# Two fifths of the second group's modulation rows moved from VectorE to TensorE, state-space operands loaded earlier, and a new order at the second norm and at the end of a hybrid block

## The chip, the cores and the metric

The kernel runs on one core of a Trainium2 chip. The metric is the device time of one execution in microseconds. Three executions of the kernel before took 1408.05, 1410.48 and 1411.93 us, so its median is 1410.48 us.

## The reference

One block over 256 tokens of width 2048, all in float32:

```
mod = silu(c) @ w_ada + b_ada                      # 2048 x 12288; six vectors of 2048
sh1, sc1, g1, sh2, sc2, g2 = split(mod, 6)
h = rms_norm(x, norm_mix_g) * (1 + sc1) + sh1
u, q, k, v, ga, gb = split(h @ w_in)               # 2048 x 8192
y_ssm = s5_branch(u, ...)                          # state space: 64 groups of 16 channels, 64 states
y_att = moba_attention(q, k, v, rel_bias)          # 8 heads of 128, with a bias table
merged = sigmoid(ga) * (y_ssm @ w_proj_ssm) + sigmoid(gb) * (y_att @ w_proj_attn)
x = x + g1 * (merged @ w_out)
h2 = rms_norm(x, norm_mlp_g) * (1 + sc2) + sh2
x = x + g2 * (square(relu(h2 @ w_ff1)) @ w_ff2)    # 2048 x 8192 and back
return rms_norm(x, norm_final_g)
```

With 256 tokens each weight is used once per token, so the kernel is a stream of weights: every matrix is read once from memory.

## The kernel before, in words

**Weight tiles.** The weights come in tiles of 128 rows by 1024 columns of float32 (512 KB), issued on SyncE's queue into `wraw`, which has 7 buffers (L130 to 132). ScalarE rounds each tile to `whi` (L137) and VectorE forms the remainder `wlo` = tile − `whi` (L139). Each has 4 buffers. TensorE then makes three products of each tile: high activations by `whi`, low activations by `whi`, high activations by `wlo`. They are L174, L175, L176 where the result is transposed (`gemm_t`, 24 products of 256 columns for a tile), L271 to L273 (`gemm_n`, 512 columns), and L232 to L234 for the product before the second norm (`gemm_h`). I count weight tiles from 0 in the order in which they are used.

**Row tiles and groups.** The 2048 rows of the contraction are 16 row tiles. The normed activations `ah` and `al` of the row tiles are made in three groups of 4, 6 and 6 (`GR`, L52), since each row tile needs its scale and shift from `w_ada` first. A list in the body (L1050 to 1052) gives the order of the products over which group: first u, q, k, v over group 0 alone, that is weight tiles 0 to 15 with four row tiles each, then longer ones over groups 0 and 1, and so on. Weight tile 20 is the first that uses row tile 4, the first of group 1.

**The modulation.** There are two ways to multiply `w_ada` by `silu(c)`. `ada_first` (L279 to 309) reads loads of w_ada from `wan`, an arrangement with the contraction on the partitions. TensorE makes four products for each load (`adap`, L299), and after four loads ScalarE copies the sums and two small products (`adac`, L306) spread them. Row tiles 0 to 3 are done so, with 16 loads, ahead of or between the first weight tiles. `ada_job` (L311 to 333) reads rows from `wat`, and VectorE multiplies and sums each load in one instruction with an accumulator (L327). Group 1 takes 24 such loads and group 2 takes 24 more, and all the other vectors follow.

**Lanes.** Beside the stream run background jobs in lanes: "ada" (loads and products of w_ada, and the making of `ah`), "ssm" (the operands of the state-space branch, L567 to 660), and others. At each weight tile a lane earns a credit, its rate (`R1`, `R2`, `R3`, `SR1`, `SR2`), and spends it on its next jobs (L118). `need(g)` (L1034) makes sure that a group's activations are there and sets the next rates. `SL` empty jobs stand at the head of the ssm lane. From the order in which the code is written, and from priorities, a scheduler fixes the order of instructions on each engine, and at run time each engine keeps to it: an instruction that waits holds up all that stand behind it on its engine.

**State space.** The operands B and C come as `bt` and `ct`, one load each on SyncE's queue (L560, L562). VectorE makes complex products of them (L581 to 583, and `rt` in L635), TensorE transposes (`trv`, L618) and multiplies (`rk`, L651).

**Second norm and end.** `gemm_h` holds the products of the second 128 tokens (t = 1) of the last row tiles back, so that TensorE has work while the first 128 tokens' norm is made; the transposes `trh` (L1199) stand among them, after the scaling L1181. The last product is w_ff2, of which the last column half keeps three row tiles (`TF`) of each result bank for the very end. Behind it stand, for each result bank, L1300 (times g2), L1301 (plus x), L1302 (square and sum, ScalarE), then `final` (L1269 to 1281): sum of the squares, root, scaling of four pieces, two on VectorE (L1280) and two on ScalarE (L1278), and their stores, all on SyncE's queue.

Of the kernel before, what the change touches and what calls it, by code (L numbers as in the profile page):

```python
# [13 lines left out]
F32R = mybir.dt.float32r  # L14
# [10 lines left out]
H = 8  # L25
# [17 lines left out]
SR1 = .3  # L43
# [3 lines left out]
SL = 6  # L47
R1 = 1.65
R2 = .95
R3 = .5  # L50
# [3 lines left out]
GR = (4, 6, 6)  # L54
RAT = 1.5
RSS = .43
RPA = .65
RWO = .45
RM = .55
NP = 4  # L60
TW = 9
TF = 3
# [12 lines left out]
class Kern:  # L75
# [132 lines left out]
    def homes(self, at, tags):  # L208
# [7 lines left out]
        for tag in tags:  # L216
            n = 2 if tag in ("VT", "QT") else 1
            for j in range(n):
                out[at] = lambda tag=tag, j=j, n=n: pair(tag, j, n)
                at += 1  # L220
        return out

    def gemm_h(self, src, kts, c0, xh, xl, homes, tail, side=3, turns=((), ())):
# [12 lines left out]
        held = []  # L236
        for i, unit in enumerate(self.stream(src, kts, c0, homes)):
            for t in range(2):
# [3 lines left out]
                for s in range(2):  # L242
                    dot(t, s, i, *unit)
        yield banks
# [6 lines left out]
        yield banks  # L251

# [26 lines left out]
    def ada_first(self, j, half, done):  # L279
        nc = self.nc  # L280
        n = 2 * (1 - j) + half
        st = {}
# [8 lines left out]
        def total(i):  # L291
# [4 lines left out]
            with self.after(None if self.early else self.mm):  # L296
                for k in range(4):
                    q = 32 * k
                    self.adap = nc.tensor.matmul(p[q:q + 32, :], self.cz[:, 4 * i + k, :], w[:, k, :], start=i == 0,  # L299
                                                 stop=i == 3, tile_position=(0, q), skip_group_check=True)  # L300
            if i == 3:
                acc = self.s4[:, 512 + 256 * n:768 + 256 * n]
                nc.scalar.copy(acc, p)
                pc = self.tmp("adac")
                for k in range(2):
                    self.adac = nc.tensor.matmul(pc[:, k:k + 1], acc[:, k * P:(k + 1) * P], self.ones[:, 0:1],  # L306
                                                 start=True, stop=True)
                done(pc[:, 0:2])
        return [(lambda i=i: load(i), lambda i=i: total(i)) for i in range(4)]
# [142 lines left out]
    def bias_load(self):  # L452
        self.tz = self.slot("T", [P, H, S], name="tz")
# [102 lines left out]
    def ssm_load_bc(self):  # L556
        self.cmp = self.slot("S5", [P, 4, 32, 16], name="cmp")
        self.ct = self.slot("RT", [P, 2, 32, 16], name="ct")
# [208 lines left out]
    def ssm_start(self):  # L767
        self.rw = self.slot("SV", [P, 4, 512], name="rw")
        self.sri = self.slot("T", [P, 2, 2, 512], name="sri")
# [86 lines left out]
    def body(self):  # L856
        nc, a, v = self.nc, self.a, self.nc.vector
        with self.hot():
# [15 lines left out]
            v.tensor_copy(self.cz[:, :, 0], rc)  # L874
            self.ident = self.col("ident", P)
# [32 lines left out]
        def modn(half):  # L908
            return (self.ada_first(1, half, fin_scale(1, A1, lambda: self.gmix, 2 * half, 2))
                    + self.ada_first(0, half, fin_shift(0, B1, 2 * half, 2)))  # L910

# [138 lines left out]
        self.hop_in()  # L1050
        self.flush("ssm")
        self.bias_load()
# [345 lines left out]
```

## Time and profile before

| | |
|---|---|
| runs | 1408.05, 1410.48, 1411.93 us |
| the profiled execution | 1411.44 us, span 1409.3 us |
| TensorE busy | 1371.2 us, 97% |
| VectorE busy | 1056.0 us, 75% |
| ScalarE busy | 706.4 us, 50% |
| read from memory | 347.27 MB |

The span goes from the first instruction to the last, and the profiled execution took 2.1 us around it. PE is TensorE, DVE is VectorE, ACT is ScalarE, POOL is GpSimd and SP is SyncE. PEld is TensorE's weight load, and an engine's name with a q is its sequencer. "Busy" counts overlapping instructions once. In a row of a group, `x` gives the number of records, then come the busy time in us and the mean of one in ns. A transposed or small fp32 product leaves two records.

### The profile page before, as it was taken

To read this page: it belongs to the slowest core of one execution; us is meant where nothing else is said; L and a number is where in the kernel's file an instruction comes from. 1 tells how busy PE (TensorE), PEld (TensorE's weight loads), DVE (VectorE), ACT (ScalarE), POOL (GpSimd) and SP (SyncE) were. 2 spreads that over 40 slices of the span, in tenths; PEclk is the share of its full clock that TensorE was granted. 3 is DMA by queue.
4 is the path that set the end of the run, shared out by engine and by line. 5 is a ranking of instruction groups with operands and counts; after the bars stand their busy time and mean duration, and the time that the engine had idled before them with its cause. 6 is when DMAs were issued, how large, how long until landed. Compare 5 with 4: busy or idle time off the path is not lost.

```text
span 1409.3 us, 23394 instructions
## 1 busy us (share of the span) xinstructions
PE 1371.2 (97%) x9258; PEld 1221.7 (87%) x9258; DVE 1056.0 (75%) x1502; ACT 706.4 (50%) x937; POOL 40.9 (3%) x94
## 2 busy tenths in 40 slices
PE   7889999999999999999999999999999999999996
PEld 6789899899999999988788888888888888888885
DVE  5788989986799888978877776767676555655676
ACT  4454343366454853455655564545463544635444
POOL 1000000320000300000000000000000000000000
PEclk9999999999999999999999999999999999999998
DMA  9999987597457988887687677777767556565551
GB/s 349 373 382 363 318 293 233 159 299 241 149 186 257 316 294 297 296 335 276 229 298 269 209 262 239 254 247 268 264 220 263 186 188 195 176 203 191 183 203 60
DMA packets 113293, 353.19 MB, mean 251 GB/s; under 512 B 12080, under 2 KB 12096, under 8 KB 113056
## 3 DMA queue, kind: packets, MB, share of 16 engines
q1 hardware_dynamic: 110384, 347.13, 70.6%
q0 software_dynamic: 2800, 4.58, 1.1%
q8 instruction: 72, 1.18, 0.3%
q14 instruction: 37, 0.30, 0.1%
HBM read 347.27 MB, written 2.29 MB: 248 GB/s over the span
## 4 chain that ended last, share of the span: by engine, by line
PE 86%; DMA 6%; DVE 5%; ACT 1%; issue 1%; SPq 0%; DVEq 0%; ACTq 0%
PE pw L202 14%; PE pn L271 10%; PE pn L273 10%; PE pn L272 10%; PE pt L174 9%; PE pt L176 9%; PE pt L175 9%; PE pw L204 7%; DMA wraw<-in_w_in_dram 3%; DVE wlo L139 2%; DVE wraw L327 1%; PE pn L233 1%; PE pn L234 1%; PE pn L232 1%; DMA wraw<-in_wat_dram 1%
## 5 line engine op out<-in xcount | busy, mean ns | idle before, releaser
L137 ACT CAST whi<-wraw 128x1024 fp32r<-128x1024 f32 x443 | 461.9, 1052 | 553.5 <-PE pn L272 177.1
L139 DVE TENSOR_TENSOR wlo<-wraw,whi 128x1024 fp32r<-128x1024 f32 x443 | 538.3, 1223 | 255.8 <-ACT whi L137 252.9
L202 PE MATMUL pw<-mh,whi 128*128 128x512 f32 x896 | 311.5, 396 | 0.2 <-DVE part L1260 0.2
L174 PE MATMUL pt<-ah,whi 128*128 128x256 f32 x896 | 251.4, 288 | 7.2 <-ACT whi L137 5.1
L175 PE MATMUL pt<-ah,whi 128*128 128x256 f32 x896 | 250.3, 285 | 0.0
L204 PE MATMUL pw<-mh,wlo 128*128 128x256 f32 x896 | 243.0, 280 | 1.0 <-DVE wlo L139 1.0
L176 PE MATMUL pt<-ah,wlo 128*128 128x256 f32 x896 | 237.7, 286 | 2.8 <-DVE wlo L139 2.5
L327 DVE SCALAR_TENSOR_TENSOR wraw<-wraw,cb 128x1024 f32<-128x1024 f32 x176 | 213.6, 1220 | 0.0
L272 PE MATMUL pn<-whi,ff 128*128 128x512 f32 x512 | 199.3, 389 | 0.0
L271 PE MATMUL pn<-whi,ff 128*128 128x512 f32 x512 | 198.6, 390 | 0.0
L202 PEld LDWEIGHTS pw<-mh,whi 128*128 128x128 f32 x896 | 165.4, 188 | 36.3 <-issue 0.5
L273 PE MATMUL pn<-wlo,ff 128*128 128x512 f32 x512 | 185.4, 389 | 0.0
L174 PEld LDWEIGHTS pt<-ah,whi 128*128 128x128 f32 x896 | 172.1, 193 | 10.8 <-ACT whi L137 6.8
L204 PEld LDWEIGHTS pw<-mh,wlo 128*128 128x128 f32 x896 | 168.8, 188 | 5.5 <-DVE wlo L139 1.4
L175 PEld LDWEIGHTS pt<-ah,whi 128*128 128x128 f32 x896 | 172.6, 193 | 0.7 <-DVE ah L139 0.2
L176 PEld LDWEIGHTS pt<-ah,wlo 128*128 128x128 f32 x896 | 164.7, 193 | 4.8 <-DVE wlo L139 4.4
L271 PEld LDWEIGHTS pn<-whi,ff 128*128 128x128 f32 x512 | 96.1, 188 | 20.0 <-issue 0.2
L273 PEld LDWEIGHTS pn<-wlo,ff 128*128 128x128 f32 x512 | 96.1, 188 | 20.1
L272 PEld LDWEIGHTS pn<-whi,ff 128*128 128x128 f32 x512 | 96.1, 188 | 19.6
L1294 DVE TENSOR_TENSOR y<-y,pn 128x512 f32<-128x512 f32 x48 | 30.9, 683 | 14.8 <-PE pn L273 14.8
L271 PE MATMUL pn<-whi,mh 128*128 128x512 f32 x96 | 37.7, 392 | 0.0
L272 PE MATMUL pn<-whi,mh 128*128 128x512 f32 x96 | 37.4, 390 | 0.0
(400 smaller groups left out, 1658.1 us busy)
## 6 DMA issues: line engine op xcount, KB each, us to landing
wraw<-in_w_ff_dram SPq DMA_DIRECT2D x256, 512.0 KB, 4.7
wraw<-in_wat_dram SPq DMA_DIRECT2D x176, 512.0 KB, 5.5
wraw<-in_w_in_dram SPq DMA_DIRECT2D x128, 512.0 KB, 5.3
wraw<-in_w_out_dram SPq DMA_DIRECT2D x32, 512.0 KB, 6.3
wraw<-in_wan_dram SPq DMA_DIRECT2D x16, 512.0 KB, 8.7
wraw<-in_w_proj_attn_dram SPq DMA_DIRECT2D x16, 512.0 KB, 6.2
wraw<-in_w_proj_ssm_dram SPq DMA_DIRECT2D x16, 512.0 KB, 5.8
wraw<-in_w_glu_dram SPq DMA_DIRECT2D x8, 512.0 KB, 5.0
```

What stands on the lines that cost most here:

```text
L137: h = self.nc.scalar.copy(hi, src)
L139: s = self.nc.vector.tensor_sub(lo, src, hi.bitcast(F32))
L174: nc.tensor.matmul(o, hi[:, c], xh[:, kx, :], start=st, stop=False, skip_group_check=True)
L175: nc.tensor.matmul(o, hi[:, c], xl[:, kx, :], start=False, stop=False, skip_group_check=True)
L176: self.mm = nc.tensor.matmul(o, lo[:, c], xh[:, kx, :], start=False, stop=sp, skip_group_check=True)
L202: nc.tensor.matmul(banks[b], hi[:, c], x2[:, k0 + k].rearrange("p h s -> p (h s)"), start=i + k == 0, stop=False, skip_group_check=True)
L204: self.mm = nc.tensor.matmul(banks[b][:, 0:S], lo[:, c], x2[:, k0 + k, 0, :], start=False, stop=i == n - 1 and k == 1, skip_group_check=True)
L271: nc.tensor.matmul(o, xh[:, kx, tk], hi[:, c], start=q == 0, stop=False)
L272: nc.tensor.matmul(o, xl[:, kx, tk], hi[:, c], start=False, stop=False)
L273: self.mm = last = nc.tensor.matmul(o, xh[:, kx, tk], lo[:, c], start=False, stop=q == n - 1)
L327: v.scalar_tensor_tensor(w, w, 1.0, self.cb[:, (i % 2) * 1024:(i % 2 + 1) * 1024], op0=OP.mult, op1=OP.mult, accum_out=pc[:, i:i + 1])
L1294: v.tensor_add(d, d, banks[b])
```

## The change

**The start.** `PP` gives the second group's row tiles 6 to 9 (as quarters 3 and 4 of the columns) to `ada_first`. 16 of the 24 loads of group 1 then go to TensorE. For these the small products are units of their own (`spread`), and the operand `cz2` and the sums lie in a new tile, `rt0`, of which `ct` takes the other part. `mod1` keeps row tiles 4 and 5. The two kinds of unit are merged evenly.

```diff
-SR1 = .3
+SR1 = .7
-SL = 6
-R1 = 1.65
+SL = 3
+R1 = 1.8
-R3 = .5
+R3 = .25
+PP = ((), (3, 4), ())
-RPA = .65
-RWO = .45
-RM = .55
+RPA = .75
+RWO = .65
+RM = .75
...
         for g in range(1, len(GR)):
             k0, n = groups[g]
-            chain += self.ahead(mod1(k0, n)) + [hjob(k0 + i) for i in range(0, n, 2)]
+            rows = mod1(k0, n - 2 * len(PP[g]))
+            cols = sum([modp(2 + sum(PP, ()).index(q), 2 * q) for q in PP[g]], [])
+            units = [u for _, _, u in sorted([((i + .5) / len(z), m, u) for m, z in enumerate((rows, cols))
+                                              for i, u in enumerate(z)], key=lambda e: e[:2])]
+            chain += self.ahead(units) + [hjob(k0 + i) for i in range(0, n, 2)]
...
-            mid = {1: lambda: second(0), 2: lambda: second(1)} if (which, g0) == (0, 0) else (lambda: need(g1)) if g1 > g0 else None
+            mid = {1: lambda: second(0), 2: lambda: second(1)} if (which, g0) == (0, 0) else {groups[g1][0] - kts[0]: lambda: need(g1)} if g1 > g0 else None
...
-        self.hop_in()
         self.flush("ssm")
         self.bias_load()
+        self.hop_in()
```

With the larger `SR1` and the smaller `SL`, the loads of `bt` and `ct` stand after weight tile 4 instead of weight tile 19. On SyncE's queue, with `in_w_in` for weight tiles and `in_wat` and `in_wan` for w_ada, this is where the two loads stood before (weight tiles 17 to 19 are the three in one row):

```order
L320 DMA wraw<-in_wat_dram 128x1024
L132 DMA wraw<-in_w_in_dram 128x1024 x3
L560 DMA cmp<-in_bt_dram 128x1024
L562 DMA ct<-in_ct_dram 128x1024
L320 DMA wraw<-in_wat_dram 128x1024
```

And this is where they stand now; the `in_w_in` row ahead of `bt` is weight tile 4:

```order
L358 DMA wraw<-in_wat_dram 128x1024
L132 DMA wraw<-in_w_in_dram 128x1024
L318 DMA wraw<-in_wan_dram 128x1024 x2
L132 DMA wraw<-in_w_in_dram 128x1024
L598 DMA cmp<-in_bt_dram 128x1024
L318 DMA wraw<-in_wan_dram 128x1024
L600 DMA rt_85<-in_ct_dram 128x1024
L358 DMA wraw<-in_wat_dram 128x1024
```

Before weight tile 20 stand 68 loads of this size in both kernels. The state-space work on VectorE moves with its operands. On VectorE, the stretch from the last product of group 1's modulation (the rows with `cb`) to the first activations of row tile 4 (`ah`) read so before:

```order
L327 SCALAR_TENSOR_TENSOR wraw,pc<-wraw,cb 128x1024 x2
L139 TENSOR_TENSOR wlo<-wraw,whi 128x1024
L429 TENSOR_TENSOR xt<-xt,R 128x512
L331 TENSOR_TENSOR pcs<-pc 128x6
L139 TENSOR_TENSOR wlo<-wraw,whi 128x1024
L429 TENSOR_TENSOR xt<-xt,R 128x512
L894 TENSOR_TENSOR B_113<-pcs,cols 128x6
L139 TENSOR_TENSOR wlo<-wraw,whi 128x1024
L635 TENSOR_TENSOR rt<-id_105,d_93 128x2048
L139 TENSOR_TENSOR ah<-htmp,ah 128x2x256
```

Now it reads as follows; L619 to L621 and L673 are state-space work:

```order
L621 TENSOR_TENSOR tt<-cmp,AB 128x512
L139 TENSOR_TENSOR wlo<-wraw,whi 128x1024
L467 TENSOR_TENSOR xt<-xt,R 128x512
L369 TENSOR_TENSOR pcs<-pc 128x2
L139 TENSOR_TENSOR wlo<-wraw,whi 128x1024
L467 TENSOR_TENSOR xt<-xt,R 128x512
L621 TENSOR_TENSOR bp<-tt 128x32x16
L937 TENSOR_TENSOR B_117<-adac,cols 128x2
L673 TENSOR_TENSOR rt<-id_109,d_97 128x2048
L937 TENSOR_TENSOR B_117<-pcs,cols 128x2
L139 TENSOR_TENSOR wlo<-wraw,whi 128x1024 x2
L365 SCALAR_TENSOR_TENSOR wraw,pc<-wraw,cb 128x1024
```

After these twelve rows come one more `wlo`, one more L365 and then `ah`. The last product of group 1's own modulation stands directly ahead of them; the two L365 belong to group 2. On TensorE, the 64 added `adap` products stand in fours and eights between weight tiles 2 and 18. The 128 `trv` transposes move from weight tiles 64 and 65 to weight tiles 29 to 44, the 128 `rk` products from weight tiles 67 and 68 to weight tiles 49 to 52.

**Slots.** `tz` (the bias table's rows), `sri` and `yl` change from the buffer "T" to "S5", `yatt` and `sg` the other way.

**Second norm.** In `gemm_h` the products held back for t = 1 are issued after the last product of the stream, and the ada lane stops for the last eleven tiles of w_out's second column half:

```diff
-            with self.after(self.turned[at[0]] if at else None):
+            with self.after(self.turned[at[0]] if at else last):
...
         for i, unit in enumerate(self.stream(src, kts, c0, homes)):
+            if i == n - tail - 2:
+                self.lanes["ada"][1] = 0.0
```

**The end.** The last column half of w_ff2's last eight row tiles goes through a new function, `gemm_e`: t = 0 is computed whole first, then t = 1 in pieces of 512, 256 and 256 columns, with the last four weight tiles kept in a larger "AHL" buffer. The steps behind the product keep their form (`last2`), so t = 0's final scaling stands ahead of t = 1's results, and two of t = 1's four stores go to ScalarE's queue.

```diff
+        first = [(self.bank("pe0"), slice(0, 512)), (self.aux("pe1"), slice(512, 1024))]
+        held = []
+        for i, unit in enumerate(self.stream(src, kts, c0, homes)):
+            held.append((i,) + unit)
+            for o, c in first:
+                dot(o, 0, c, *held[-1])
+        last = self.mm
+        yield first
+        then = []
+        for name, c in (("pe2", slice(0, 512)), ("pe3", slice(512, 768)), ("pe4", slice(768, 1024))):
+            o = (self.aux(name) if name == "pe3" else self.bank(name))[:, 0:c.stop - c.start]
+            for u in held:
+                dot(o, 1, c, *u, last=last)
+            then.append((o, c))
+        yield then
...
-                nc.sync.dma_start(self.out[0, t * P:(t + 1) * P, cc], o)
+                    q = nc.sync if t == 0 or c in (0, 2) else nc.scalar
+                    q.dma_start(self.out[0, t * P:(t + 1) * P, cc], o)
```

VectorE's rows before, from the last result bank (`pn_13461`) to the sum of t = 1's squares; L399 to L402 are the small steps of t = 0's root:

```order
L1300 TENSOR_TENSOR y_9010<-pn_13461,g2b 128x512
L399 RECIPROCAL r30s<-r30s 128x1
L1301 TENSOR_TENSOR x<-x,y_9010 128x512
L400 SCALAR_TENSOR_TENSOR r30t<-r30s 128x1
L401 TENSOR_TENSOR r30t<-r30t,r30v 128x1
L402 SCALAR_TENSOR_TENSOR r30s<-r30t,r30s 128x1
L1280 SCALAR_TENSOR_TENSOR x<-x,r30s,gfb 128x512 x2
L1272 TENSOR_REDUCE fs_13637<-fq 128x1
```

And now, where `r30s` is the root of t = 0, `r31s` that of t = 1, and `pe_13701` the last piece of 256 columns:

```order
L1331 SCALAR_TENSOR_TENSOR x<-x,r30s,gfb 128x512 x2
L1339 TENSOR_TENSOR y_9087<-pe_13651,g2b 128x512
L1340 TENSOR_TENSOR x<-x,y_9087 128x512
L1339 TENSOR_TENSOR y_9087<-pe_13676,g2b 128x256
L1340 TENSOR_TENSOR x<-x,y_9087 128x256
L1339 TENSOR_TENSOR y_9087<-pe_13701,g2b 128x256
L1340 TENSOR_TENSOR x<-x,y_9087 128x256
L1323 TENSOR_REDUCE fs_13735<-fq 128x1
```

The two scalings of t = 0 stood between the last result and the sum of its squares, and now stand ahead of all of t = 1's results.

More of the change, by code (lines that the diff above doesn't have):

```diff
@@ L251, in gemm_h, with gemm_e, dot @@
         yield banks
+    def gemm_e(self, src, kts, c0, xh, xl, homes, koff):
+        nc = self.nc
+        n = len(kts)
+        def dot(o, t, c, i, kt, hi, lo, last=None):
+            tk, kx = slice(t * P, (t + 1) * P), kt - koff
+            with self.after(last):
+                nc.tensor.matmul(o, xh[:, kx, tk], hi[:, c], start=i == 0, stop=False)
+            nc.tensor.matmul(o, xl[:, kx, tk], hi[:, c], start=False, stop=False)
+            self.mm = nc.tensor.matmul(o, xh[:, kx, tk], lo[:, c], start=False, stop=i == n - 1)
+        first = [(self.bank("pe0"), slice(0, 512)), (self.aux("pe1"), slice(512, 1024))]
[4 more added lines that the diff above has]
+                dot(o, 0, c, *held[-1])
+        last = self.mm
+        yield first
[6 more added lines that the diff above has]
+        yield then
     def gemm_n(self, src, kts, c0, xh, xl, koff=0, tail=1):
@@ L281, in ada_first @@
         n = 2 * (1 - j) + half
+        cz = self.cz if half < 2 else self.cz2
         st = {}
@@ L298, in total, with spread @@
                     q = 32 * k
-                    self.adap = nc.tensor.matmul(p[q:q + 32, :], self.cz[:, 4 * i + k, :], w[:, k, :], start=i == 0,
+                    self.adap = nc.tensor.matmul(p[q:q + 32, :], cz[:, 4 * i + k, :], w[:, k, :], start=i == 0,
                                                  stop=i == 3, tile_position=(0, q), skip_group_check=True)
             if i == 3:
-                acc = self.s4[:, 512 + 256 * n:768 + 256 * n]
-                nc.scalar.copy(acc, p)
-                pc = self.tmp("adac")
-                for k in range(2):
[L306 to L309, printed above, removed]
+                st["acc"] = (self.s4[:, 512 + 256 * n:768 + 256 * n] if half < 2 else
+                             self.rt0[:, 1536 + 256 * j:1792 + 256 * j])
+                nc.scalar.copy(st["acc"], p)
+                if half < 2:
+                    spread()
+        def spread():
+            pc = self.tmp("adac")
+            with self.after(None if half < 2 else self.mm):
+                for k in range(2):
+                    self.adac = nc.tensor.matmul(pc[:, k:k + 1], st["acc"][:, k * P:(k + 1) * P],
+                                                 (self.ones if half < 2 else self.one)[:, 0:1], start=True, stop=True)
+            done(pc[:, 0:2])
+        units = [(lambda i=i: load(i), lambda i=i: total(i)) for i in range(4)]
+        return units if half < 2 else units + [(lambda: None, spread)]
     def ada_job(self, vec, k0, n, done):
@@ L1265, in ff1 @@
                     self.split(f[:, 0, s], f[:, 1, s], fr[:, s])
-        fq = self.col("fq", 8)
+        fq = self.col("fq", 9)
         def final(t):
@@ L1280, in final, with last2 @@
                         v.scalar_tensor_tensor(o, o, rf, gfb[:, cc], op0=OP.mult, op1=OP.mult)
[L1281 removed]
+                    q = nc.sync if t == 0 or c in (0, 2) else nc.scalar
+                    q.dma_start(self.out[0, t * P:(t + 1) * P, cc], o)
+        def last2(t, o, c, q, keep=None):
+            keep = keep or (lambda ins: ins)
+            d = acc[:, t, c]
+            with self.hot():
+                keep(v.tensor_mul(d, o, g2b[:, c]))
+                keep(v.tensor_add(x1[:, t, c], x1[:, t, c], d))
+                nc.scalar.activation(d, x1[:, t, c], AF.Square, accum_out=fq[:, q:q + 1])
         def ff2(g):
             f = ffs.pop(g)
[L1285 to L1287 removed]
+            for cg in range(1 if g == 7 else 2):
+                banks = self.gemm_n(w2, range(8 * g, 8 * g + 8), cg * 1024, f[:, 0], f[:, 1], koff=8 * g)
                 for b in range(4):
```

51 lines of the change are left out of this document (27 added, 24 removed).

## The prediction

> **What bounds the kernel now.** I read the page first, then the windows of the first 380 us, then the chain and TensorE's timeline where a window shows loss. The page says that TensorE sets the time almost everywhere:
>
> ```profile
> PE 1371.2 (97%) x9258; PEld 1221.7 (87%) x9258; DVE 1056.0 (75%) x1502; ACT 706.4 (50%) x937; POOL 40.9 (3%) x94
> ```
>
> So the change can save only what TensorE idles, what it does at a lower clock, and the tail behind it. The windows of the start show where that is (columns: window, its length, busy time of PE, PEld, DVE, ACT, POOL, granted clock, DMA share, GB/s):
>
> ```profile
> 42.00:104.00 62.00, 55.48 (x387) 50.12 (x388) 53.67 (x75) 29.23 (x41) 0.00 (x0) 1.00 1.01 387
> 104.00:192.00 88.00, 83.51 (x603) 79.29 (x603) 78.75 (x112) 37.76 (x43) 0.00 (x0) 0.96 0.87 317
> 192.00:380.00 188.00, 184.73 (x1900) 179.26 (x1899) 155.36 (x232) 95.17 (x154) 19.65 (x40) 0.98 0.71 232
> ```
>
> Up to 104 us the DMA is full (1.01) and TensorE idles 6.5 of 62 us. From 104 to 192 us VectorE is nearly full, 78.75 of 88, and TensorE idles 4.5. From 192 to 380 us VectorE has 32.6 us to spare, TensorE idles 3.3 us and runs at a clock of 0.98. The borders are weight tiles, by the timeline of TensorE (start, duration): weight tiles 20, 48 and 100 are first used with their `wlo` at
>
> ```profile
> 104.17 0.39 PE L176 MATMUL pt<-ah,wlo 128*128 128x256 f32 x1
> 192.09 0.28 PE L176 MATMUL pt<-ah,wlo 128*128 128x256 f32 x1
> 380.16 0.28 PE L176 MATMUL pt<-ah,wlo 128*128 128x256 f32 x1
> ```
>
> I count the sum in these three times, which I call T20, T48 and T100. After T100 the streams are alike until the second norm.
>
> **The start, up to weight tile 20.** The prices of an instruction among its like are in the chain (start, duration) and the groups:
>
> ```profile
> L299 PE MATMUL adap<-wraw,tz 128*32 128x256 f32 x128 | 8.2, 384 | 0.9 <-DMA wraw<-in_wan_dram 0.8
> 38.42 0.62 PE adac L306 x4
> 742.58 1.23 DVE wraw L327 x2
> 743.81 1.15 DVE wlo L139
> 240.20 1.13 DVE tt L583
> 249.75 0.61 DVE tt L583
> ```
>
> VectorE loses 16 L327 at 1.23 us, 19.7 us. TensorE gains as many `adap` as it has now, 8.2 us, and four groups of `adac` at 0.62: 10.7 us. That is 4.2 more than the 6.5 it idles there, so by TensorE alone T20 would be at most 104.2 + 4.2 = 108.4. The number of loads before weight tile 20 stays 68, so the full DMA lands that tile at the same time. What decides is VectorE's order. Now, by its timeline, the activations of row tile 4 follow 9.3 us behind the start of group 1's last L327, and `rt` in between waits 1.07 us for ScalarE's copy of `ct`:
>
> ```profile
> 93.02 1.22 DVE L327 SCALAR_TENSOR_TENSOR wraw<-wraw,cb 128x1024 f32<-128x1024 f32 x1
> 100.09 2.29 DVE L635 TENSOR_TENSOR rt<-id,d 128x2048 f32<-128x2048 f32 x1 [1.07 <-ACT cc L567]
> 102.30 0.68 DVE L139 TENSOR_TENSOR ah<-htmp,ah 128x512 fp32r<-128x512 f32 x1
> ```
>
> The early operands take that wait away. But in the new order there stand between the same two places five wlo, two L327 of group 2, two state-space steps, `rt` and two `xt`: 5 x 1.15 + 2 x 1.23 + 0.61 + 0.61 + 2.29 + 2 x 0.61 = 12.9 us, 13.5 with the smallest. The last load of group 1 is number 63 in the order of loads, 61 before; a load of 524 KB at 387 GB/s takes 1.35 us, so its L327 starts at about 95.7 and ends at 96.9. `ah` then starts at 110.4. The other bound is the load of weight tile 22, number 71, whose wlo stands ahead of `ah`: three loads (4.1 us) behind weight tile 20, whose wlo starts at
>
> ```profile
> 102.98 1.14 DVE wlo L139
> ```
>
> which is 101.9 without the wait of 1.07 before `rt`. Then 101.9 + 4.1 + 1.15 + 1.23 = 108.4 is the least for `ah`. If that wait stays, 110.4 becomes 111.5, about 112. I take 110 for `ah` and so for T20, 6 us later than now. TensorE then waits some 2 to 6 us at weight tile 20, which it does not do now. Now it waits one tile later:
>
> ```profile
> 108.81 0.39 PE L176 MATMUL pt<-ah,wlo 128*128 128x256 f32 x1 [1.49 <-DVE wlo L139]
> ```
>
> **From weight tile 20 to 48.** VectorE's new order holds, from `ah` to weight tile 48's wlo, 26 wlo (29.9 us), 22 L327 (27.1), 12 state-space steps of 1.13 (13.6), and 29 short ones at 0.61 (12 more state-space steps, 12 evacuations, 5 on `xt` and `ah`: 17.7), together 88.3, with the smallest some 88.5. The old order filled 78.75. TensorE needs 83.51 at a clock of 0.96, 80.2 at full clock, and the transposes moved here:
>
> ```profile
> L618 PE MATMUL trv<-ident,bp 64*64 64x64 f32 x256 | 7.9, 219 | 0.0
> ```
>
> That is 88.1, so TensorE and VectorE are level here, and any idle of VectorE counts. It idles 9.25 of 88 us now, for loads among other things:
>
> ```profile
> 151.20 8.25 DMA wraw<-in_w_in_dram
> 159.56 1.06 ACT whi L137
> 160.66 0.58 PE pt L174
> ```
>
> I take 2 us of idle, because a fuller VectorE leaves loads more time (ends: 0 and all 9.25), and 1.5 for TensorE's half tile behind it. T48 = 110 + 88.5 + 2 + 1.5 = 202.0, against 192.1: 9.9 us later.
>
> **From 48 to 100: paid back.** The transposes are gone from here, 7.9 us. VectorE's work falls from 155.4 to about 120 us by the same count, while TensorE's is 184.73 x 0.98 − 7.9 = 173, so VectorE is not late for the `rk` products as it is now:
>
> ```profile
> 255.00:260.00 5.00, 1.73 (x13) 1.41 (x12) 4.97 (x5) 1.58 (x4) 0.00 (x0) 0.81 0.00 0
> 260.00:266.00 6.00, 6.00 (x126) 5.78 (x124) 5.15 (x9) 2.69 (x5) 0.00 (x0) 0.59 0.78 244
> ```
>
> The chain leads through L581 to L583 into ScalarE's L641 and then to `rk`. TensorE idles 3.3 us of the first window, then runs 6 us at 0.59, which loses 2.5: 5.8 in all. The loads start earlier, so VectorE's results lie ready and I count the whole 5.8 as gone. Sum: 7.9 + 5.8 = 13.7. T100 is 9.9 − 13.7 = **3.8 us earlier**. With other ends: `ah` at 108.5 and no idle give −7.3; `ah` at 112 and 5 us of idle give +1.2. The two removed waits, on `ct` and at `rk`, are thus mostly bought with a new one at weight tile 20.
>
> [...] First the rows: after waits of 0.26, 0.76 and 1.98 us TensorE ran at 0.51 for 6 us,
>
> ```profile
> 155.00:160.00 5.00, 2.66 (x13) 1.66 (x11) 4.16 (x8) 1.49 (x2) 0.00 (x0) 0.91 1.03 415
> 160.00:166.00 6.00, 5.34 (x25) 5.35 (x26) 6.00 (x9) 2.70 (x3) 0.00 (x0) 0.51 0.89 309
> 160.66 0.58 PE L174 MATMUL pt<-ah,whi 128*128 128x256 f32 x1 [1.98 <-ACT whi L137]
> ```
>
> so a spell costs 6 x 0.49 = 2.9 us, and the new wait at weight tile 20 should bring one. TensorE's 88.1 and these 2.9 are 91.0, within the 92.0 us from 110 to 202, so it adds nothing to the sum; in A it adds 2.9 at most. [...]
>
> **Slots, bias table, other rates.** Moving `tz`, `sri`, `yl`, `yatt` and `sg` between two buffers, and the bias table ahead of `hop_in` on GpSimd's queue, I cost at nothing: GpSimd is 3% busy. If a buffer came free late, TensorE would wait a few us before 400 us; this lies in the range.
>
> **Second norm.** TensorE waits 1.17 us at the first transposes:
>
> ```profile
> 678.55 0.50 DVE xs L1181
> 679.18 1.06 PE L1199 MATMUL trh<-ident,xs 128*128 128x128 f32 x8 [1.17 <-DVE xs L1181]
> ```
>
> VectorE is late there by its L327. In the new order no L327 stands among the last eleven splits of w_out, where six stood: 7.4 us less on VectorE, more than the 1.17. The transposes should not wait, with what the pipeline refills −1.3. The L327 left out come later, where this chain shows VectorE as the last to end (two of its rows, 742.58 and 743.81, stand above); if they press there, 1 us comes back.
>
> **The end.** After TensorE's last product the chain now reads
>
> ```profile
> 1398.37 0.69 DVE y L1300
> 1399.13 0.66 DVE x L1301
> 1400.28 1.42 DVE x L1280 x2
> 1401.69 0.08 DVE fs L1272
> ```
>
> and in the timeline ScalarE's square and the eight stores are
>
> ```profile
> 1399.82 0.63 ACT L1302 ACTIVATE y<-x 128x512 f32<-128x512 f32 x1 [1.22 <-DVE x L1301]
> 1401.06 4.50 SPq L1281 DMA_DIRECT2D out_dram<-x  x8
> ```
>
> The sum of squares of t = 1 waits for t = 0's scaling, 1.42 us, and comes 1401.69 − 1398.37 = 3.3 us behind the product. In the new order that scaling is done earlier, and the last piece has 256 columns, so the three steps 0.69, 0.66 and 0.63 take somewhat over half, and with the accumulator's read some 1.7: −1.6. TensorE pays: 24 products of 512 columns become 48 of 256. Their steps are
>
> ```profile
> 1397.20 0.23 PE pn L272
> 1397.42 0.23 PE pn L273
> 380.04 0.28 PE L175 MATMUL pt<-ah,whi 128*128 128x256 f32 x1
> ```
>
> 0.227 us over many such rows, and 0.12 (to 380.16): 48 x 0.12 − 24 x 0.227 = +0.3. Eight stores take 4.50 us to issue, 0.56 each with its wait; two of the last four on another queue save about half of one, −0.3. Sum −1.6. `gemm_e` needs t = 0's last weights no later than now, and keeps four tiles, so I see no new wait; if there is one, TensorE waits 1 to 2 us.
>
> **The sum.** −3.8 − 1.3 − 1.6 = −6.7. The profiled execution took 1411.4 us and would take 1404.7; it lies 0.96 above the median of 1410.48, and against that I predict **1403.8 us**. A measurement of this kernel can tell about 0.3% from no change, 4.2 us: below 1406.3 is faster, above 1414.7 slower.
>
> **The rivals.**
> - Forecast, 0.48: VectorE sets T48, rests after it, and the sum is 1400 to 1407.
> - A, larger gain, 0.17: `ah` comes near 105, because VectorE, relieved of 19.7 us, runs through its rows as loads land. Then TensorE is the bound: T48 = 105 + 88.1 = 193, one us later than now, and less 13.7 the start gives −12.7; in all −15.6, 1394.9, with 1392 to 1398. For it: VectorE's 53.67 of 62 us loses more than a third. Against it: the new order puts weight tile 22's wlo ahead of `ah`.
> - B, moved only, 0.22: the change doesn't do what it says, since VectorE's state-space work lands in the stretch where it was nearly full. `ah` at 112 and 5 to 6 us of idle make T48 207.5 to 208.5, and the start +2: 1409.6, with 1406 to 1413. For it: the 78.75 of 88.
> - C, slower, 0.13: VectorE's idle does not shrink, because the loads arrive as late as now and every split waits behind an L327 that waits for its load. With `ah` at 114 and all 9.25 us of idle, T48 is 213.3, 21 later; less 13.7 the start is +7.5 and the total +4.6: 1415. It decides from about 9 us of idle on. For it: a DMA share of 0.87 there. Against it: the total of loads is unchanged, and 22 L327 take the place of 24.
>
> Faster is A and most of the forecast, 0.60; same the rest of it and B, 0.27; slower C, 0.13. The range leaves out C and the far part of A: 1394 to 1413.
>
> **What would show it.** In the profile after: a first use of weight tile 20 near 110 us with a wait on `ah` or its wlo; VectorE over 85 of 88 us busy from there to weight tile 48; no wait at `rk`, and a clock near 1.00 from T48 to T100; weight tile 100 at 376; the wait at `trh` gone; some 1.7 us from the last product to the last sum of squares. I am wrong if T20 stays near 104 (A), or if VectorE idles over 5 us between weight tiles 20 and 48 (B, C).

## The result, and the profile after

The changed kernel takes 1422.91 us (median of 4), against 1409.57 for the kernel before on the same chip: a ratio of 1.0093, interval 1.008 to 1.0106. It is slower by some 13 us, 0.9%, and 1 lies outside the interval; 1403.8 was forecast and 1413 was the upper end. (16 of group 1's 24 loads moved, which is two thirds of the second group's rows and not the two fifths of the title.) The profiled execution took 1422.08 us (span 1420.2), 10.6 us more than that of before; the page of the kernel after begins its busy times with

```profile
PE 1385.2 (98%) x9426; PEld 1227.4 (86%) x9426; DVE 1038.8 (73%) x1479; ACT 706.4 (50%) x944; POOL 41.3 (3%) x95
```

VectorE is relieved, by 17 us, as the change says, and TensorE is busy 14 us more. To see where the time went I mark the moments by which TensorE has done 20, 53, 69, 101, 200 and 250 weight tiles' worth of products. Lateness of the kernel after at these marks: 7.4, 28.9, 6.4, 6.4, 8.0 and 10.6 us; at TensorE's last product 12.2, and at the end of the span 10.9. The 28.9 is mostly the state-space products, which now lie ahead of mark 53 and not behind it. Windows between the first marks, of the kernel before (window, length, busy PE, PEld, DVE, ACT, POOL, clock, DMA share, GB/s):

```profile
0.00:103.10 103.10, 86.14 (x626) 72.88 (x627) 73.76 (x180) 47.02 (x68) 5.29 (x21) 0.98 0.98 371
103.10:205.40 102.30, 97.81 (x722) 93.59 (x721) 92.49 (x128) 46.26 (x54) 0.00 (x0) 0.97 0.88 321
205.40:274.00 68.60, 65.33 (x899) 64.11 (x898) 65.83 (x90) 25.29 (x32) 4.73 (x10) 0.95 0.63 208
```

and of the kernel after:

```profile
0.00:110.50 110.50, 95.27 (x769) 77.73 (x770) 63.81 (x166) 48.20 (x70) 5.76 (x22) 0.97 0.94 349
110.50:234.30 123.80, 119.22 (x1234) 111.02 (x1233) 112.48 (x153) 55.41 (x72) 4.22 (x8) 0.97 0.80 266
234.30:280.40 46.10, 46.10 (x387) 46.10 (x386) 30.98 (x36) 16.76 (x16) 0.82 (x2) 1.00 0.72 228
```

Summed up to mark 69, TensorE is busy 249.3 us before and 260.6 after, 11.3 more, and idles 24.7 us before and 19.8 after, 4.9 less: together the 6.4. The 11.3 are the added products, by their groups:

```profile
L330 PE MATMUL adap<-wraw,rt 128*32 128x256 f32 x128 | 9.4, 388 | 0.0
L343 PE MATMUL adac<-one,rt 128*128 128x1 f32 x16 | 2.0, 229 | 0.0
```

The prediction counted on 6.5 us of idle time that TensorE has from 42 us on, and let the added products fill it. From 42 us to mark 20 TensorE still idles 3.4 us, and up to mark 20 in all its idle time falls by 1.7 only, from 17.0 to 15.2. For the last 29 us ahead of mark 20 it does not idle at all:

```profile
81.30:110.50 29.20, 29.20 (x247) 26.68 (x248) 22.58 (x31) 12.08 (x16) 0.00 (x0) 0.94 0.91 338
```

The DMA's share up to mark 20 falls from 0.98 to 0.94. What holds the loads back is seen in what SyncE's queue waits for before it issues a weight tile's load. The first row is the kernel before up to mark 20, the second the kernel after (us in total, times, longest):

```profile
SPq L132 <- PE adap L299: 1.1, 2, 0.7
SPq L132 <- PE adap L330: 17.8, 10, 3.2
```

A load of w_ada that goes to TensorE keeps its buffer of `wraw` until its `adap` products are done, and ten weight tiles wait for such a buffer. After mark 20 TensorE waits twice, by its timeline:

```profile
113.00 0.74 PE L174 MATMUL pt<-ah,whi 128*128 128x256 f32 x4 [2.18 <-ACT ah L137]
116.14 0.58 PE L175 MATMUL pt<-ah,whi 128*128 128x256 f32 x1 [2.40 <-DVE ah L139]
```

VectorE's timeline shows what stands ahead of that `ah`; the first L365 is the last of group 1, the other two belong to group 2:

```profile
100.33 1.23 DVE L139 TENSOR_TENSOR wlo<-wraw,whi 128x1024 fp32r<-128x1024 f32 x1 [2.61 <-ACT whi L137]
101.47 1.22 DVE L365 SCALAR_TENSOR_TENSOR wraw<-wraw,cb 128x1024 f32<-128x1024 f32 x1
...
107.44 2.28 DVE L673 TENSOR_TENSOR rt<-id,d 128x2048 f32<-128x2048 f32 x1
109.64 0.15 DVE L937 TENSOR_TENSOR B<-pcs,cols 128x2 f32<-128x2 f32 x1
109.71 2.35 DVE L139 TENSOR_TENSOR wlo<-wraw,whi 128x1024 fp32r<-128x1024 f32 x2
111.98 1.21 DVE L365 SCALAR_TENSOR_TENSOR wraw<-wraw,cb 128x1024 f32<-128x1024 f32 x1
...
114.26 1.22 DVE L365 SCALAR_TENSOR_TENSOR wraw<-wraw,cb 128x1024 f32<-128x1024 f32 x1
...
115.40 0.68 DVE L139 TENSOR_TENSOR ah<-htmp,ah 128x512 fp32r<-128x512 f32 x1
```

and the windows of TensorE around it show the clock:

```profile
112.00:116.10 4.10, 0.74 (x4) 0.53 (x4) 4.10 (x8) 1.87 (x3) 0.00 (x0) 0.92 0.84 283
116.10:123.00 6.90, 6.86 (x35) 6.86 (x36) 6.83 (x11) 4.27 (x7) 0.00 (x0) 0.55 0.94 353
```

VectorE has no gap between 101.47 and 115.40, and waited 2.61 us for a conversion just before; the load of that weight tile was issued at 93.92, when an `adap` had freed its buffer. So this one place costs 4.6 us of wait and about 3 us (6.9 x 0.45) of clock, and uses up what the wait at the `rk` products gives back, which is gone as forecast (idle 3.3 us from mark 53 to 69 before, 0.0 after).

The prediction's T20, the first product with `wlo` of weight tile 20, is here

```profile
116.52 0.41 PE L176 MATMUL pt<-ah,wlo 128*128 128x256 f32 x1
```

and its T48 and T100, by the same rows, 211.80 and 386.58. The window from T20 to T48 shows TensorE busy for all of it, and VectorE not:

```profile
116.50:211.80 95.30, 95.30 (x854) 88.11 (x854) 87.11 (x118) 40.40 (x51) 0.00 (x0) 0.97 0.79 279
```

### The profile page after: what moved, and what is told of

Same layout as the page of the kernel before. It is cut to its first block, busy times and chain, and to the rows that moved or that the text cites. A ratio compares the mean times of both kernels' runs of the same rounds, so it can differ in the third digit from the quotient of the medians.

```text
span 1420.2 us, 23697 instructions
## 1 busy us (share of the span) xinstructions
PE 1385.2 (98%) x9426; PEld 1227.4 (86%) x9426; DVE 1038.8 (73%) x1479; ACT 706.4 (50%) x944; POOL 41.3 (3%) x95
## 4 chain that ended last, share of the span: by engine, by line
PE 83%; DVE 7%; DMA 5%; ACT 2%; issue 2%; DVEq 0%; SPq 0%; ACTq 0%
PE pw L202 13%; PE pt L174 9%; PE pt L176 9%; PE pt L175 9%; PE pn L301 9%; PE pn L302 9%; PE pn L303 9%; PE pw L204 6%; DVE wlo L139 3%; DVE wraw L365 2%; DMA wraw<-in_w_ff_dram 1%; DMA wraw<-in_w_out_dram 1%; DMA wraw<-in_w_in_dram 1%; PE pn L234 1%; PE pn L232 1%
## 5 line engine op out<-in xcount | busy, mean ns | idle before, releaser
L139 DVE TENSOR_TENSOR wlo<-wraw,whi 128x1024 fp32r<-128x1024 f32 x439 | 532.7, 1221 | 283.6 <-ACT whi L137 276.2
L137 ACT CAST whi<-wraw 128x1024 fp32r<-128x1024 f32 x439 | 457.1, 1051 | 557.3 <-PE pn L302 164.7
L174 PE MATMUL pt<-ah,whi 128*128 128x256 f32 x896 | 255.5, 290 | 6.1 <-ACT ah L137 4.3
L175 PE MATMUL pt<-ah,whi 128*128 128x256 f32 x896 | 254.7, 287 | 2.4 <-DVE ah L139 2.4
L176 PE MATMUL pt<-ah,wlo 128*128 128x256 f32 x896 | 248.6, 287 | 0.0
L365 DVE SCALAR_TENSOR_TENSOR wraw<-wraw,cb 128x1024 f32<-128x1024 f32 x160 | 194.5, 1217 | 0.0
L302 PE MATMUL pn<-whi,ff 128*128 128x512 f32 x480 | 186.9, 389 | 0.0
L301 PE MATMUL pn<-whi,ff 128*128 128x512 f32 x480 | 185.9, 390 | 0.0
L175 PEld LDWEIGHTS pt<-ah,whi 128*128 128x128 f32 x896 | 174.8, 195 | 3.1 <-DVE ah L139 2.8
L303 PE MATMUL pn<-wlo,ff 128*128 128x512 f32 x480 | 173.1, 389 | 0.0
L176 PEld LDWEIGHTS pt<-ah,wlo 128*128 128x128 f32 x896 | 170.8, 195 | 0.6
L301 PEld LDWEIGHTS pn<-whi,ff 128*128 128x128 f32 x480 | 90.1, 188 | 18.9 <-issue 0.2
L303 PEld LDWEIGHTS pn<-wlo,ff 128*128 128x128 f32 x480 | 90.0, 188 | 18.6
L302 PEld LDWEIGHTS pn<-whi,ff 128*128 128x128 f32 x480 | 90.1, 188 | 18.3
```

The lines of the kernel that those rows point to most:

```text
L137: h = self.nc.scalar.copy(hi, src)
L139: s = self.nc.vector.tensor_sub(lo, src, hi.bitcast(F32))
L174: nc.tensor.matmul(o, hi[:, c], xh[:, kx, :], start=st, stop=False, skip_group_check=True)
L175: nc.tensor.matmul(o, hi[:, c], xl[:, kx, :], start=False, stop=False, skip_group_check=True)
L176: self.mm = nc.tensor.matmul(o, lo[:, c], xh[:, kx, :], start=False, stop=sp, skip_group_check=True)
L301: nc.tensor.matmul(o, xh[:, kx, tk], hi[:, c], start=q == 0, stop=False)
```

## The experiments

Each is told with its edit, the text on record, the ratio to the kernel before on the same chip, and its lateness at the marks against the profiled execution of before. Repeated starts of the same code differ by 1 to 3 us at the marks (the kernel after stands at 6.4 at mark 69, the same start in `start_alone` at 9.3), so I read differences below that from no single trace.

**Parts alone.** `start_alone` is the kernel after with the second norm, `RPA`, `RWO`, `RM` and the end as before.

> The whole change at the start (TensorE's w_ada loads, early state-space operands, rates, slots), with the second norm and the end as before. Theory 1, that the start is where most is lost: some 6 us slower than before (1416), with TensorE 6.4 us late at weight tile 100 and no more from there on than now. Rival, that the start pays for itself and the second norm and the end lose the time: within 2 us of before.

1.0122 (1.0105 to 1.0139), +9.3 us at mark 69, +10.2 at mark 200, +18.7 at mark 250. The start is where the loss begins, and without the raised rates another 8.5 us are lost behind mark 200. That was in neither expectation.

`products_alone` and `ssm_early_alone` each take half of the start, by one more edit to `start_alone`:

```diff
-SR1 = .7
-SL = 3
+SR1 = .3
+SL = 6
```

> The w_ada products of row tiles 6 to 9 on TensorE, with the state-space operands as late as before (rates SR1 .3, SL 6). Theory 1, that TensorE's added 11 us of products are not hidden: 5 to 10 us slower than before, since the wait of 5.8 us at the rk products stays and the transposes stay late. Rival, that VectorE's relief of 16 products is worth more and the early state-space work in VectorE's order is what makes row tile 4 late: 3 to 6 us faster than before, weight tile 20 used before 108 us.

```diff
-PP = ((), (3, 4), ())
+PP = ((), (), ())
```

> The state-space operands early (SR1 .7, SL 3), with all 24 w_ada loads of group 1 on VectorE as before. Theory 1: the wait at the rk products goes (5.8 us), TensorE has no added products, but VectorE has the state-space work on top of the 16 products in a stretch where it was nearly full, so row tile 4 is later still; within 5 us of before, on the slower side. Rival, that the added TensorE products are the only loss: 4 to 6 us faster than before.

1.0091 (1.0073 to 1.011) and 1.0037 (1.0024 to 1.005). At mark 69 they stand at −0.6 and −2.6, at mark 101 at −0.6 and −1.2, then at mark 250 at +10.2 and +2.7. Each half of the start is free by itself in these traces, which spoke against my theory 1, that the products always cost; together they cost 6.4. In `products_alone` TensorE's idle time up to mark 69 falls by 8.5 us, so there the products do find room. But both lose later. The reason is in the loads of w_ada, counted on SyncE's queue by the time of the 200th weight tile's load; the modulation needs 162 by the 240th:

| kernel | w_ada loads at weight tile 200 | TensorE's loss between marks 200 and 250, us |
|---|---|---|
| before | 144 | 0 |
| after | 139 | 2.6 |
| start_alone | 136 | 8.5 |
| products_alone | 136 | 9.8 |
| ssm_early_alone | 139 | 3.3 |
| second_norm_alone | 148 | −1.2 |

The later the w_ada loads, the more of their products fall on VectorE beside the first products of w_ff1 and the second norm. In `products_alone` the transposes of the second norm wait again, longer than before:

```profile
679.52 1.06 PE L1248 MATMUL trh<-ident,xs 128*128 128x128 f32 x8 [2.43 <-DVE xs L1230]
693.60 1.07 PE L1248 MATMUL trh<-ident,xs 128*128 128x128 f32 x8 [1.99 <-DVE xs L1230]
```

`second_norm_alone` is the kernel before with `gemm_h`, `RPA`, `RWO` and `RM` of the change.

> The second norm's part alone (held products after the last of the stream, ada lane stopped for the last weight tiles of w_out, rates RPA .75, RWO .65, RM .75), all else as before. Theory 1: the waits of 1.3 us at the first transposes and of 1.2 us at 745 us go, but the raised rates put w_ada products ahead of the sums of the first w_ff1 products, where six waits of 0.5 to 0.7 us appear, so 2 to 4 us slower. Rival, that this comes from the changed start: 1 to 2 us faster than before.

1.0000 (0.9991 to 1.0009). The transposes do not wait (−1.35 us from mark 195 to 200), and 2.4 us are lost ahead of them, at the start of w_out, where w_ada loads crowd in at the raised rates. It is neither theory: no loss at w_ff1, and no gain.

**Rates and order.** `rate_back` puts one number back into the kernel after, `rates_of_before` two:

```diff
-R3 = .25
+R3 = .5
```

> The kernel after with one number put back: R3 .5 as before instead of .25, so that the ada lane does not fall behind once all of group 2 is there. Theory 1, that the late w_ada loads pile up behind the second norm: TensorE loses nothing between weight tiles 150 and 250, where the kernel after lost 4.3 us, so some 4 us faster than after. Rival, that those waits come from the ada lane's stop and the raised rates alone: no change, within 1.5 us of after.

```diff
-R3 = .25
+R3 = .5
-RM = .75
+RM = .55
```

> The kernel after with R3 .5 and RM .55 as before. If the raised rate crowds VectorE at the first w_ff1 products, the 2.7 us lost between weight tiles 200 and 250 fall below 1 and the whole is 2 to 3 us faster than after. Rival, that the ada lane's stop for the last weight tiles of w_out shifts the load there whatever the rate: no change.

`rate_back` 1.0079 (1.0061 to 1.0097), `rates_of_before` 1.0048 (1.0032 to 1.0064). `R3` alone cures nothing behind mark 200 (+2.8 us there). With `RM` back as well, TensorE gains 1.0 us between marks 200 and 250, and the ratio falls by 0.3%. VectorE's w_ada products between these marks are in the kernel after and in `rates_of_before`

```profile
L365 DVE SCALAR_TENSOR_TENSOR wraw<-wraw,cb 128x1024 f32<-128x1024 f32 x26 | 31.4, 1217 | 0.0
```
```profile
L365 DVE SCALAR_TENSOR_TENSOR wraw<-wraw,cb 128x1024 f32<-128x1024 f32 x19 | 22.9, 1218 | 0.0
```

and TensorE's waits for the sums of the first w_ff1 products, in the same order:

```profile
PE pw L202 <- DVE part L1382: 2.2, 5, 0.5
```
```profile
PE pw L202 <- DVE part L1382: 0.5, 1, 0.5
```

So neither number alone cures the loss behind mark 200: `start_alone` has `RM` of before and loses 8.5, `rate_back` has `R3` of before and loses 2.8. `rate_back` has 19 of the products there too, but three more of the loads come by weight tile 220 (159 against 156), and TensorE waits there mostly for `wlo` and not for sums. The raised `RM` alone does no harm where the loads are further on: `second_norm_alone` has it, and 148 loads by weight tile 200.

`row4_first` puts three empty units into the ada lane, so that the two L365 of group 2 stand behind row tile 4's `ah`:

```diff
-            chain += self.ahead(units) + [hjob(k0 + i) for i in range(0, n, 2)]
+            chain += self.ahead(units) + [hjob(k0 + i) for i in range(0, n, 2)] + [lambda: None] * 3 * (g == 1)
```

> The kernel after with three empty units in the ada lane between group 1 and group 2, so that two w_ada products of group 2 stand behind, not ahead of, the activations of row tile 4 on VectorE. Theory 1, that VectorE's order makes row tile 4 late: ah ends 2.4 us earlier, near 113.5 instead of 116, TensorE waits 2 to 3 us less at weight tile 20, and weight tile 69 comes 2 to 5 us earlier than in the kernel after. Rival, that TensorE's products set it: weight tile 69 as in the kernel after, within 1 us.

1.0080 (1.0062 to 1.0098). TensorE is 1.3 us less late at weight tile 22 (12.1 against 13.4), but at weight tile 45 later than the kernel after (21.2 against 20.4), and at mark 69 stands at 6.4, as it does. What the order gives at one group it takes at the next, whose loads start three weight tiles later.

`ssm_sooner` has `SR1 = 1.4`, so that nearly all state-space work stands ahead of that `ah`.

> The kernel after with SR1 1.4 instead of .7, so that nearly all state-space work on VectorE stands ahead of the activations of row tile 4. Theory 2, that VectorE idles before weight tile 20 (28.7 of 50 us busy from 50 to 100) and is full after it, so the relief comes in the wrong stretch: the work moved into the idle time is free, weight tile 69 comes 3 to 5 us earlier than in the kernel after. Rival, that whatever stands ahead of those activations delays them: weight tile 20 another 3 us or more later, and weight tile 69 not earlier.

1.0089 (1.0073 to 1.0105). Weight tile 21 is 24.7 us late instead of 14.3, and mark 69 5.9 instead of 6.4: the rival's first half, and then no difference. Three very different orders on VectorE end at the same 6 us, so its order ahead of row tile 4 is not what sets mark 69. `half_products` gives TensorE half of the loads:

```diff
-PP = ((), (3, 4), ())
+PP = ((), (4,), ())
```

> The kernel after with only row tiles 8 and 9 on TensorE (8 of the 24 loads instead of 16). Theory 2: TensorE's added work falls to 5.5 us and weight tile 20 comes 2 to 4 us earlier than in the kernel after, weight tile 69 2 to 4 us earlier. Rival, that only the order ahead of row tile 4's activations counts: weight tile 69 within 1.5 us of the kernel after.

1.0031 (1.0019 to 1.0044), mark 20 at +3.9 and mark 69 at −0.75, 7.2 us earlier than the kernel after, twice what I expected. So with eight loads on TensorE mark 69 is no later than before, and the second eight cost 7.2 us.

**TensorE's work taken away.** `products_thinned` leaves out 36 of the 64 added products, so it does not compute the modulation; all other engines have the same order as in the kernel after.

```diff
-                for k in range(4):
+                for k in range(1 if i and half > 1 else 4):
```

> The kernel after, leaving out 36 of the 64 added adap products (of each load after a group's first only one of four is made, so the sums are not the reference's); loads, buffers and the order on all other engines stay. Theory 3, that TensorE's added work is paid in full because TensorE is the bound: weight tile 20 comes 3 to 4 us earlier than in the kernel after, and weight tile 69 and the whole 3 to 4 us earlier. Rival, that the loads held until TensorE reaches them, or VectorE's order, set the time: weight tile 69 within 1 us of the kernel after.

Its windows between the first marks are

```profile
0.00:109.20 109.20, 95.02 (x698) 77.00 (x698) 63.78 (x166) 48.12 (x70) 5.75 (x22) 0.98 0.95 354
109.20:231.60 122.40, 117.72 (x1234) 109.53 (x1233) 112.52 (x153) 55.35 (x72) 4.22 (x8) 0.99 0.81 269
231.60:277.70 46.10, 46.10 (x386) 46.10 (x385) 30.96 (x36) 16.78 (x16) 0.81 (x2) 1.00 0.70 228
```

TensorE's busy time up to mark 20 is 95.02 us, where the kernel after has 95.27: leaving out the products took almost no time off TensorE. The timelines show why. The first three rows are a load with its four products in the kernel after, the last three a load with one of the four:

```profile
44.41 0.28 PE L176 MATMUL pt<-ah,wlo 128*128 128x256 f32 x1
44.62 0.64 PE L330 MATMUL adap<-wraw,rt 128*32 128x256 f32 x8
45.19 0.38 PE L174 MATMUL pt<-ah,whi 128*128 128x256 f32 x1
```
```profile
47.30 0.28 PE L176 MATMUL pt<-ah,wlo 128*128 128x256 f32 x1
47.51 0.62 PE L330 MATMUL adap<-wraw,rt 128*32 128x256 f32 x2
48.06 0.38 PE L174 MATMUL pt<-ah,whi 128*128 128x256 f32 x1
```

From the product ahead to the product behind it is 0.78 us with four and 0.76 with one. So the run is no test of theory 3, though it was meant as one. Its timed ratio, 1.0090 (1.0073 to 1.0108), is that of the kernel after, and the 2.7 us by which mark 69 comes earlier are within what two starts of the same code differ by.

`ssm_full` takes all 64 products off TensorE, and their VectorE work is back: no products on TensorE, operands early, `R3 = .5`, the second norm's part with its rates, and the mended end (below).

> The state-space operands early, all of group 1's w_ada loads on VectorE, R3 .5, the second norm's part with all its rates, and the mended end. Theory 3: 0 to 1 us gained by weight tile 101, no wait of 4 us before the second norm now that the ada lane is further on, 1.4 us gained at the end: 1 to 3 us faster than before. Rival: within 1 us of before or slower.

1.0004 (0.9994 to 1.0014). Its windows between the first marks:

```profile
0.00:107.90 107.90, 87.22 (x626) 74.24 (x627) 84.51 (x199) 47.15 (x67) 5.75 (x22) 0.95 0.97 362
107.90:226.50 118.60, 115.77 (x1235) 107.85 (x1234) 114.37 (x157) 55.00 (x70) 4.21 (x8) 1.00 0.86 294
226.50:272.60 46.10, 46.10 (x386) 46.10 (x386) 35.46 (x48) 16.78 (x16) 0.88 (x2) 1.00 0.85 271
```

This is the cleanest pair with `rate_back`, which differs in the products and the end only: 1.0004 against 1.0079. VectorE does 234.3 us of work up to mark 69, 27 more than in the kernel after, and TensorE is there at 272.6 us, 7.8 earlier. TensorE is busy 249.1 us, as before the change, and idles 23.5.

`products_caught_up` (products, late operands, `R3 = .5`, the change's second norm, mended end) and `ssm_caught_up` (as `ssm_full`, with `RPA` and `RWO` as before) complete the set.

> The w_ada products on TensorE with the state-space operands as late as before, R3 .5 as before, the second norm's part of the change, and the mended end. Theory 2, that early operands and products only hurt together and that a late ada lane costs some 9 us behind the second norm: weight tile 101 within 1.5 us of before, at most 2 us lost between weight tiles 150 and 250, 1.4 us gained at the end; within 2 us of before. Rival, that the added products cost their 11 us somewhere: over 5 us slower than before.

> The state-space operands early, all of group 1's w_ada loads on VectorE, R3 .5, RPA and RWO as before, RM .75 and the order of the second norm as in the change, and the mended end. Theory 2: 1 to 2 us gained by weight tile 101, about 1 us at the second norm, 1.4 us at the end, nothing lost behind the second norm: 2 to 4 us faster than before. Rival: the late w_ada loads still cost 2 us or more between weight tiles 150 and 250, so no faster than before.

1.0058 (1.0042 to 1.0074) and 1.0044 (1.0029 to 1.006). The first stands at +1.2 at mark 69, once its `rk` products are done, and at +6.9 at mark 101, with waits of 3.5 us in between that `products_alone` does not have, the longest, 2.7, for ScalarE ahead of transposes of the attention branch. The total is the rival's; what makes these waits I have not followed. The second loses some 6 us between marks 150 and 195, ahead of the second norm, 4.0 of them in one wait for a weight tile's conversion. `ssm_full`, with the higher rates, has no such wait; the two differ in nothing else.

**The end.** `end_alone` is the kernel before with `gemm_e` and what belongs to it.

> The end's part alone (gemm_e, the order of the last steps, two queues for the stores), all else as before. Theory 1: the tail behind TensorE's last product is 1.4 us shorter, but TensorE waits 1.3 us for the last wlo, which stands behind the evacuation of the first column half on VectorE, and its smaller pieces cost 0.35: within 1 us of before. Rival, as predicted: 1.3 us faster, no wait.

1.0009 (0.9998 to 1.0019). TensorE waits 1.87 us for the last wlo and is 3.8 us later behind it (the smaller pieces not counted), since its clock falls as well. Timeline and window:

```profile
1381.84 0.73 PE L261 MATMUL pe<-wlo,ff 128*128 128x512 f32 x2 [1.87 <-DVE wlo L138]
```
```profile
1382.00:1388.00 6.00, 6.00 (x20) 4.77 (x21) 4.01 (x7) 1.95 (x6) 0.00 (x0) 0.72 0.00 0
```

In the kernel after it is the same wait, shorter and without the fall of the clock (1.00 from 1393 to 1397 us):

```profile
1393.19 0.73 PE L265 MATMUL pe<-wlo,ff 128*128 128x512 f32 x2 [1.30 <-DVE wlo L139]
```

and the chain of the kernel after shows VectorE's order ahead of it, the evacuation of the first column half:

```profile
1389.53 1.88 DVE y L1339 x3
1391.47 0.45 issue
1391.92 1.23 DVE wlo L139
1393.19 0.73 PE pe L265 x2
```

`end_mended` puts that evacuation behind the last wlo:

```diff
+                first = next(halves)
+                for b in range(4):
+                    t, c = b // 2, slice(b % 2 * 512, b % 2 * 512 + 512)
+                    with self.after(self.done[-5][0]):
+                        last2(t, banks[b], c, t * 4 + b % 2)
```

> The end's part alone, with the evacuation of the first column half placed behind the last wlo on VectorE. Theory 1: TensorE's wait of 1.3 us goes, and the end is 1.0 to 1.4 us faster than before. Rival, that the last wlo is late for its load or its buffer: the wait stays.

The wait is gone. The chain of `end_mended` from the last product's evacuation on:

```profile
1398.53 0.44 DVE y L1314
1398.99 0.44 DVE x L1315
1399.45 0.52 ACT y L1316 x2
1399.99 0.17 DVE fs L1298
```

1399.99 − 1398.53 is 1.46 us, where it took 1401.69 − 1398.37 = 3.3 before; the span is 1407.8 against 1409.3. The timed ratio, 0.9995 (0.9985 to 1.0004), cannot tell it from no change. `norm_and_end` joins this end and the change's second norm.

> The kernel before with the second norm's part of the change and the mended end, and the start as before. Theory 3: no cost at the start, about 1 us gained at the second norm and 1.4 us at the end: 1.5 to 3 us faster than before. Rival, that the raised rates lose at w_out what they gain: within 1 us of before.

1.0000 (0.9990 to 1.0010), the rival. No version that I ran beats the kernel before beyond its interval.

## Why the prediction was wrong

- **TensorE's added products as covered, and VectorE as the bound of the start: the step that failed.** The prediction took 6.5 of TensorE's added 10.7 us as covered ("6.5 it idles there") and let T48 follow from VectorE's order. Measured: of these 6.5 us only 3.1 were filled, TensorE paid most of its 11.3 us, and from 81.30 to 110.50 us it never idled. The rest of the idle time was no room here: it is time in which TensorE waits for a weight tile's conversion (all of the 3.4 us that are left from 42 us to mark 20), and the weight tiles' loads now wait for buffers that `adap` frees (17.8 us up to mark 20, 1.1 before). `ssm_full` against `rate_back` shows that with the operands early the products cost some 0.7%, and that VectorE could do them (the ends differ too; `end_mended` puts that at 0.05%); `half_products`, with half of them, has mark 69 no later than before. That `products_alone` is not late at mark 69 shows that the cost comes from products and early operands together; how the two divide it stays open.
- **T20 was forecast at 110 and measured at 116.5** by the same row (`wlo` of weight tile 20), 4.5 us above the upper end of 112. VectorE's part was right: from group 1's last L365 to `ah` it took 13.9 us (101.47 to 115.40), where 14.7 were counted. But that L365 started at 101.5 and not at 95.7. I had derived its start from a load every 1.35 us, with the DMA as full as before; it stood behind a `wlo` whose load was issued late, for a buffer that `adap` held. This is the first step's mistake again.
- **From T20 to T48 TensorE was the bound, not VectorE.** It took 95.3 us (211.8 − 116.5), where 92.0 were forecast. TensorE has no idle time there and VectorE has 8.2 us, where 2 were counted and over 5 was named as a sign of being wrong. The prediction put TensorE's own need at 88.1 and 2.9 for a spell at the low clock, 91.0 in all, and let VectorE cover it. The spell was the right size (about 3). The transposes were not: by the starts in the timelines, `trv` took 7.9 us in two stretches before, and takes 11.7 us in 16 stretches among the weight tiles' products now. These 3.8 us more are most of what the 95.3 have over the 91.0.
- **From 48 to 100: right.** Forecast −13.7, measured 174.8 us against 188.1, −13.3. The wait at `rk` and its slow clock are gone (clock 1.00 from mark 53 to 69, 0.95 before), the transposes have moved. With the steps above, T100 was forecast 3.8 us earlier and was 6.4 later.
- **Rates "at nothing": the second step that failed.** The paragraph headed "Slots, bias table, other rates" costs them at nothing and gives no reason for the rates. `R3` at .25 puts the ada lane behind (139 loads at weight tile 200, with .5 in `rate_back` 146), and `RM` at .75 packed the rest at w_ff1. From mark 101 to mark 250 the kernel after loses 4.2 us: 3.0 ahead of the second norm, 2.6 behind it, less the 1.35 gained there. `rates_of_before` shows it: 1.0048 against 1.0093, and no loss behind mark 200.
- **Second norm: right** in place and size: no wait at the transposes, −1.3 forecast, −1.35 measured. The "1 us that comes back" was 2.6, and the 3.0 ahead of it, between marks 150 and 195, had no term.
- **The end: right in its terms, wrong in the supply.** The tail went from 11.0 to 9.6 us behind TensorE's last product, −1.35, and the smaller pieces cost +0.35, as counted. I saw "no new wait" and named 1 to 2 us if there were one; it was 1.3, so the end gave nothing.
- Rival C had the sign and a third of the size (+4.6 forecast, +13 measured), for the wrong reason. Its `ah` near 114 and VectorE's idle time of about 9 us nearly came (115.4 and 8.2), but TensorE was busy throughout that stretch, so this idle time did not decide. (By its own terms, B's T48 is 207.0 to 208.0; nothing hangs on it.)

## What to carry to other kernels

Idle time on the engine that bounds a kernel is room for more work only as far as the added work leaves its supply alone: where that idle time is a wait for loads, count what the added work does to their buffers, or count it in full (3.1 of the 6.5 us were room in this kernel). Small products among large ones cost more here than the same products in one stretch: `trv` takes 11.7 us against 7.9. Relief of another engine is worth nothing unless a wait on it ends last, in the stretch where the relief falls: VectorE has 17 us less to do in the kernel after, which is 13 us slower. And a rate that starts background work later is not free because the stretch it leaves is calm; look for where the work must be done by, and what stands there.

## What the runs showed of the hardware

What TensorE's clock did behind waits: after 1.30 us, at the end of the kernel after, it stayed at 1.00 (1393 to 1397 us), and after 1.87 us at the same place in `end_alone` it fell to 0.72 over 6 us, which is 1.7 us lost. In the kernel after, two waits of 2.18 and 2.40 us with 0.74 us of work between them left it at 0.55 over the next 6.9 us. Full pitch returned at 122.3, 6.1 us after work resumed at 116.14. After a wait of 1.88 us, work resumed at 81.30 and the clock was 0.50 over the next 3.4 us, then 1.00 over 3.3 us. The length of the last wait alone did not decide whether the clock fell: behind the waits of 2.43 and 1.99 us at the second norm in `products_alone` the products of 512 columns follow each other every 0.23 to 0.24 us from the second on, as they do at a clock of 1.00 behind the wait of 1.17 us there in the kernel before.

Four small products of 32 columns between two weight tiles cost TensorE 0.66 us in the kernel after (at 44.62 us) where eight cost 1.09 (at 85.84), so the change to them and back is about 0.2 us each time, an estimate: 0.66 less the 0.43 that four more cost. In `products_thinned` one product in place of four costs 0.64 us, so leaving out three of the four saved next to nothing.
